# 128 bytes ahead of three phases' buffers, three half tiles instead of four, the last turn inside the third, two more edges of order

## The chip, the cores and the metric

The kernel runs on one core of one Trainium2 chip. The metric is the device time of one execution in microseconds, the median over several runs. A core has a matrix engine (TensorE; PE in the profile, with its weight loads as PEld), a vector engine (VectorE, DVE), a scalar engine (ScalarE, ACT), GpSimd (POOL), and a sync engine (SP), which here issues all loads and stores. Each engine works through a queue of its own in a fixed order, and semaphores hold the queues together.

## The reference

A trunk of two layers for 512 tokens of 1024 channels, all in float32. Layer 0 mixes tokens with a Mamba-2 state space mixer, layer 1 with HGRN2. Behind either mixer stand a layer norm, a squared-ReLU MLP of 4096 hidden channels, another layer norm and a gated input of per-layer embeddings:

```python
for i in range(DEPTH):
    mix = ssd_mixer(x, ...) if i % 2 == 0 else hgrn2_mixer(x, ...)
    h = layer_norm(DEEPNORM_ALPHA * x + mix, ln_g[i, 0], ln_b[i, 0])
    h = layer_norm(DEEPNORM_ALPHA * h + sq_relu_mlp(h, mlp_w1[i], mlp_w2[i]), ln_g[i, 1], ln_b[i, 1])
    x = h + jax.nn.sigmoid(h @ ple_w_gate[i]) * (p[i] @ ple_w_proj[i])

def sq_relu_mlp(h, w1, w2):
    a = jax.nn.relu(h @ w1)
    return (a * a) @ w2
```

In the mixer of layer 0, `u @ w_in` gives the columns x (16 tiles of 128 channels), z (16 tiles), B, C and dt; x, B and C pass a causal convolution of width 4 and a silu before the chunked state computation.

## The kernel before

**Products in three passes.** A float32 product is made of three matmuls in a faster float32 mode. Both factors are split into a high part, rounded by ScalarE (`nc.scalar.copy`), and a low part, the rest, taken by VectorE (`tensor_sub`). `mm3` (lines 117 to 120) issues high by high, high by low and low by high. A weight tile of 128x1024 is loaded by SP into one of three `raw` buffers and split into one of six `whi` and one of six `wlo` buffers; `unit` (line 101) does the load and `split` (108) the rest. The trace names the operand that moves through the array first and the one that is held in it second: `pj<-b,whi` moves an activation past held weights (`project`, line 135), `pj<-whi,b` moves weights past a held activation, 128 tokens of it at a time (`out_part`, `product`, the gate). `pj`, `py`, `pt` and `pm` are the banks of PSUM.

**Buffers.** The pools lie in SBUF in the order in which they are opened: constants, `raws`, `whip`, `wlop`, `b8`, `accp`, `w4`, `sm`, and behind them the pool of the phase (`begin`, line 74), whose buffers are replaced at each of the four phases ssd, mlp0, hgrn and mlp1. The buffers of `raws`, `whip`, `wlop` and `w4` hold 4096 bytes in each partition, those of `b8` 8192, `acc` 16384, so all of these start at the same remainder of 4096. The small tiles of `sm` take 640 bytes (one name of 2x64 and eight of 2x32), and the phase's first buffer begins right behind them. In the two MLP phases it is `blk`, two buffers of 8192 bytes that hold the activation blocks `s3` and `s4`; the other five blocks (`a11`, `a12`, `a22`, `s1`, `s2`) lie in `b8`.

**MLP.** `mlp_and_gate` works on the hidden channels in four groups `g`. `hidden(g)` makes 16 tiles of them in two rounds `p` and lays the squared activations down in seven blocks for a product by Strassen's scheme; `block_product` (337) multiplies these with sums of the second weight matrix (`weight_sums`, 313, buffers `r`). Seven products of 24 matmuls belong to a group; two of the seven (`p7` and `p3`) hold `s3` and `s4`.

**From mixer to MLP in layer 0.** `out_project` with `spread` interleaves the last projection of the mixer with the layer norm of the four chunks of 128 tokens (`layer_norm`, 197, ending with line 213 on VectorE) and with the turn of each chunk (`transpose_split`, 215): eight transposes on TensorE (222), two casts on ScalarE (227), two subtractions on VectorE (228). Chunks 0 and 1 are turned inside `out_project`. Chunks 2 and 3 are handed on as `turns`: the first four tiles of the MLP (`g == p == 0`) are projected for tokens 0 to 255 alone, the turn of chunk 2 follows behind the second of these halves and that of chunk 3 behind the fourth, and then the four second halves follow for tokens 256 to 511.

**What sets the order.** A list scheduler orders each engine's queue when the program is built, by the order of the program text, by priorities (`tc.high_priority`) and by its own estimate of times. TensorE's order in the mixers is written out by hand (`manual_schedule`). `behind(ins)` (97) adds an edge of order: what the block issues on the engine of `ins` comes behind `ins` in that engine's queue. No semaphore belongs to it, and instructions of the block on other engines are free. `marks["pe"]` is the last matmul that was issued, `marks["norm", 0]` the last VectorE instruction of the latest chunk's layer norm.

**The start of layer 0.** `x_part(j)` (625) projects column tile j of x, passes it through `conv_silu` (577: ScalarE's line 580, three additions on VectorE in line 583, a silu on ScalarE in line 586) and keeps the last addition in `conv[j][0]`. Behind tiles x0, z0, x1 and z1, `turn_pair(0)` (646, transposes in line 652) needs the silu of tiles 0 and 1. Then `x_part(2)` follows on TensorE.

Of the kernel before, what the change touches and what calls it, by code (L numbers as in the profile page):

```python
# [15 lines left out]
P = 128  # L16
T = 512
# [24 lines left out]
def trunk(ctx: ExitStack, tc, a):  # L42
    nc = tc.nc
# [14 lines left out]
    uid, marks = [0], {}  # L58
# [16 lines left out]
    def begin(name):  # L75

        if phase:
            phase[1].__exit__(None, None, None)
            phase.clear()
        phase.append(tc.tile_pool(name=name, bufs=1, reuse_waits="tile"))  # L80
        phase.append(phase[0].__enter__())
        phase.reverse()
        phase.append(bufs[name])

    def tmp(tag, shape, dt=F32):
        return mk(phase[0], shape, tag, dt, bufs=phase[2].get(tag, 1))
# [11 lines left out]
    def behind(ins):  # L98
        return nullcontext() if ins is None else tc.issue_after(ins.ins)
# [17 lines left out]
    def mm3(out, sh, sl, mh, ml, start, stop, **kw):  # L117
        nc.tensor.matmul(out, sh, mh, start=start, stop=False, **kw)  # L118
        nc.tensor.matmul(out, sh, ml, start=False, stop=False, **kw)  # L119
        marks["pe"] = nc.tensor.matmul(out, sl, mh, start=False, stop=stop, **kw)  # L120
# [11 lines left out]
        def l(self, k, sl=slice(0, T)):  # L132
            return self.lo[k // 4][:, k % 4, sl]

    def project(src, xs, ps, m=P, tok=slice(0, T)):

        hi, lo = src
        for k in range(8):
            c = slice(k * m, (k + 1) * m)
            mm3(ps[:m, tok], hi[:, c], lo[:, c], xs.h(k, tok), xs.l(k, tok), k == 0, k == 7)  # L140


    begin("ssd")
# [243 lines left out]
    def mlp_and_gate(layer, h_s, last, turns=()):  # L387

        w1, w2 = a[f"w1_{layer}"], a[f"w2_{layer}"]
        blocks = {}  # L390

        def hidden(g):
            names = ("a11", "a12", "a22", "s1", "s2", "s3", "s4")
            blocks[g] = {
                n: tmp("blk", [P, 2, 4, 256], F32R) if n in ("s3", "s4") else mk(b8, [P, 2, 4, 256], "b8", F32R)
                for n in names
            }
            for p in range(2):
                tiles = [4 * (2 * g + r) + 2 * p + i for r in range(2) for i in range(2)]
                us = []  # L400
                if g == p == 0:
                    for i, m in enumerate(tiles):
                        us.append((unit(w1[m]), bank(psj, "pj")))
                        project(us[-1][0], h_s, us[-1][1], tok=slice(0, 256))
                        if turns and i % 2:
                            with behind(marks["pe"]):
                                turns[i // 2]()
                zs = []
                for r in range(2):
                    z = mk(w4, [P, 2, T], "ab"[r])  # L410
                    for i in range(2):
                        if us:
                            u, ps = us[2 * r + i]
                            project(u, h_s, ps, tok=slice(256, 512))
                        else:
                            ps = bank(psj, "pj")
                            with behind(marks["norm", 0] if (layer, g, p, r, i) == (0, 0, 1, 0, 0) else None):
                                u = unit(w1[tiles[2 * r + i]])
                            project(u, h_s, ps)
                        nc.scalar.activation(z[:, i], ps, AF.Relu)  # L420
                        if i == 1:
                            nc.scalar.activation(z, z, AF.Square)
                            zs.append(z)
                            if r == 1:
                                half_blocks(blocks[g], *zs, p)
                        yield

        for g, period in enumerate(PERIODS):
            if g < 4:
                tiles = hidden(g)  # L430
            if g > 0:
                if g == 4:
                    h_s, after, turned, sums = norm(2 * layer + 1)
                    p_s = (mk(w4, [P, 2, T], "a", F32R), mk(w4, [P, 2, T], "b", F32R))
                    praw = mk(raws, [P, 1024], "raw")
                    nc.sync.dma_start(praw, a[f"pT_{layer}"].rearrange("p k t -> p (k t)"))
                    praw = praw.rearrange("p (k t) -> p k t", k=2)
                    nc.scalar.copy(p_s[0], praw)
                    nc.vector.tensor_sub(p_s[1], praw, f32(p_s[0]))
                w = [[[w2[8 * g - 8 + 4 * i + 2 * j + u] for u in range(2)] for j in range(2)] for i in range(2)]  # L440
                products = block_product(w, blocks.pop(g - 1), SUMS[g - 1], g == 1, *((after, lambda: turned(0), sums) if g == 4 else ()))
            for op in period:
                next(tiles if op == "T" else products)

        x_n = None if last else Split(8)
        late = []

        def turn(h, c):

            sl = slice(c * P, (c + 1) * P)  # L450
            pt = bank(psm, "pm") if c % 2 else bank(pst, "pt")
            for j in range(4):
                nc.tensor.transpose(pt[:, j * P : (j + 1) * P], acc[:, c, h * 512 + j * P : h * 512 + (j + 1) * P], ident)
            v = pt.rearrange("p (j t) -> p j t", j=4)
            hh = x_n.hi[h][:, :, sl]
            nc.scalar.copy(hh, v)
            nc.vector.tensor_sub(x_n.lo[h][:, :, sl], v, f32(hh))

        pps = {}

        def proj(c, pu):

            pp = pps[c] = bank(*((psj, "pj") if c > 1 and pps else (psy, "py%d" % (c % 2))))
            for k in range(2):
                ks = slice(k * 512, (k + 1) * 512)
                mm3(pp, p_s[0][:, k, c * P : (c + 1) * P], p_s[1][:, k, c * P : (c + 1) * P], pu[0][:, ks], pu[1][:, ks], k == 0, k == 1)

        for h in range(2):
            pu = unit(a[f"wp_{layer}"][h])
            gu = [unit(a[f"wg_{layer}"][4 * h + j]) for j in range(4)]  # L470
            for c in range(NCH):
                sl = slice(c * P, (c + 1) * P)
                if h == c == 0:
                    for i in range(NCH):
                        proj(i, pu)
                        if i == 1:
                            turned(1)
                if h == 1:
                    proj(c, pu)
                pp = pps.pop(c)  # L480
                pg = bank(psj, "pj")
                sg = tmp("sg", [P, T])
                parts = 2 if last and h == 1 and c == NCH - 1 else 1
                for i in range(parts):
                    n = 512 // parts
                    if i:
                        pg = bank(psj, "pj")
                    cs = slice(i * n, (i + 1) * n)
                    for k in range(8):
                        ks = slice((k % 2) * 512 + i * n, (k % 2) * 512 + (i + 1) * n)  # L490
                        mh, ml = gu[k // 2][0][:, ks], gu[k // 2][1][:, ks]
                        mm3(pg[:, cs], h_s.h(k, sl), h_s.l(k, sl), mh, ml, k == 0, k == 7)
                        if h == 0 and c < 2 and k == 2:
                            turned(c + 2)
                    nc.scalar.activation(sg[:, cs], pg[:, cs], AF.Sigmoid)
                    nc.vector.tensor_mul(sg[:, cs], pp[:, cs], sg[:, cs])
                    fs = slice(h * 512 + i * n, h * 512 + (i + 1) * n)
                    d = acc[:, c, fs]
                    nc.vector.tensor_add(d, sg[:, cs], d)
                    if last:  # L500
                        nc.sync.dma_start(a["out"][c * P : (c + 1) * P, fs], d)
                while late:
                    late.pop(0)()
                if not last:
                    late.append(lambda h=h, c=c: turn(h, c))
        return x_n, late
# [3 lines left out]
    ps = bank(psj, "pj")  # L510
# [79 lines left out]
    def projected(i):  # L590

        if i < 2:
            return first[i]
        ps = bank(psj, "pj")
        project(unit(wssd[i - 2]), x_s, ps)
        return ps
# [26 lines left out]
    prep, live, decay, pair, conv = {}, {}, {}, {}, {}  # L623

    def x_part(j):
        ps = projected(10 * (j // 4) + 2 + 2 * (j % 4))
        xs = tmp("xs", [P, T])
        conv[j] = conv_silu(ps, j, xs)
        live[j] = [xs]
# [135 lines left out]
    with tc.manual_schedule(engines={mybir.EngineType.PE}):  # L765
# [8 lines left out]
        for k in range(1, 9):  # L774
            i, j = 2 * k, 2 * k + 1
# [540 lines left out]
```

## Time and profile before

| | us |
|---|---|
| median of 3 runs | 1421.09 (1419.85 to 1421.74) |
| the profiled execution | 1420.3 |
| its span, first to last instruction | 1418.4 |
| TensorE busy | 1412.2 |
| VectorE busy | 1019.1 |
| ScalarE busy | 741.7 |

A group's row in the profile gives line, engine, operation, tiles and shape, the count, the busy time in us and the mean record of one instruction in ns. Records of matmuls overlap their successors, since the array is pipelined: what one matmul costs is the distance from its start to the next one's start, which is read in the timeline, whose rows begin with a start and a length in us.

### The profile page before, as it was taken

To read this page: it belongs to the slowest core of one execution; us is meant where nothing else is said; L and a number is where in the kernel's file an instruction comes from. 1 tells how busy PE (TensorE), PEld (TensorE's weight loads), DVE (VectorE), ACT (ScalarE), POOL (GpSimd) and SP (SyncE) were. 2 spreads that over 40 slices of the span, in tenths; PEclk is the share of its full clock that TensorE was granted. 3 is DMA by queue.
4 is the path that set the end of the run, shared out by engine and by line. 5 is a ranking of instruction groups with operands and counts; after the bars stand their busy time and mean duration, and the time that the engine had idled before them with its cause. 6 is when DMAs were issued, how large, how long until landed. Compare 5 with 4: busy or idle time off the path is not lost.

```text
span 1418.4 us, 20300 instructions
## 1 busy us (share of the span) xinstructions
PE 1412.2 (100%) x8063; PEld 1181.4 (83%) x8063; DVE 1019.1 (72%) x1677; ACT 741.7 (52%) x1099; POOL 1.5 (0%) x8
## 2 busy tenths in 40 slices
PE   9999999999999999999999999999999999999998
PEld 7888888888988888888888888888898888888887
DVE  7997777695877667687854775676785857666873
ACT  7786566473464444545533446465554454544551
POOL 0000000000000000000000000000000000000000
PEclk9999999999999999999999999999999999999999
DMA  8524333322444444442422322221263444444231
GB/s 296 167 84 134 108 101 119 105 93 102 169 131 146 142 141 141 141 140 98 156 83 92 105 90 74 85 96 63 74 223 111 150 140 142 141 138 160 89 119 45
DMA packets 48958, 174.81 MB, mean 123 GB/s; under 512 B 5728, under 2 KB 6368, under 8 KB 48736
## 3 DMA queue, kind: packets, MB, share of 16 engines
q1 hardware_dynamic: 48864, 173.52, 36.7%
q8 instruction: 63, 1.03, 0.3%
q14 instruction: 31, 0.25, 0.1%
HBM read 171.34 MB, written 2.16 MB: 122 GB/s over the span
## 4 chain that ended last, share of the span: by engine, by line
PE 97%; DVE 1%; DMA 1%; ACT 1%; issue 0%; SPq 0%; ACTq 0%
PE pj L118 25%; PE pj L119 25%; PE pj L120 25%; PE py L118 5%; PE py L119 5%; PE py L120 5%; PE py L709 1%; PE py L975 1%; PE py L711 1%; PE pt L222 1%; PE pt L692 0%; PE pm L222 0%; DVE cv L583 0%; DMA raw<-in_wssd 0%; DMA acc<-in_xw 0%
## 5 line engine op out<-in xcount | busy, mean ns | idle before, releaser
L112 ACT CAST whi<-raw 128x1024 fp32r<-128x1024 f32 x226 | 236.9, 1050 | 386.0 <-PE pj L119 270.3
L114 DVE TENSOR_TENSOR wlo<-raw,whi 128x1024 fp32r<-128x1024 f32 x226 | 274.1, 1220 | 194.5 <-ACT whi L112 191.8
L118 PE MATMUL pj<-b,whi 128*128 128x512 f32 (+1 forms) x1008 | 381.1, 379 | 0.2 <-ACT b L227 0.2
L119 PE MATMUL pj<-b,whi 128*128 128x512 f32 (+1 forms) x1008 | 378.9, 376 | 0.0
L120 PE MATMUL pj<-b,wlo 128*128 128x512 f32 (+1 forms) x1008 | 378.8, 376 | 0.0
L120 PE MATMUL pj<-whi,b 128*128 128x512 f32 (+1 forms) x592 | 229.1, 387 | 0.0
L118 PE MATMUL pj<-whi,b 128*128 128x512 f32 (+1 forms) x584 | 228.8, 392 | 0.0
L119 PE MATMUL pj<-wlo,b 128*128 128x512 f32 (+1 forms) x584 | 226.0, 387 | 0.0
L120 PEld LDWEIGHTS pj<-b,wlo 128*128 128x128 f32 x1008 | 189.7, 188 | 34.4
L118 PEld LDWEIGHTS pj<-b,whi 128*128 128x128 f32 x1008 | 189.5, 188 | 34.6 <-ACT b L227 0.5
L119 PEld LDWEIGHTS pj<-b,whi 128*128 128x128 f32 x1008 | 189.8, 188 | 34.2 <-DVE b L228 0.2
L120 PEld LDWEIGHTS pj<-whi,b 128*128 128x128 f32 x592 | 111.2, 188 | 22.8 <-DVE b L1170 0.2
L118 PEld LDWEIGHTS pj<-whi,b 128*128 128x128 f32 x584 | 109.7, 188 | 23.1 <-ACT k L904 0.4
L119 PEld LDWEIGHTS pj<-wlo,b 128*128 128x128 f32 x584 | 109.8, 188 | 21.3
L112 ACT CAST whi<-r 128x1024 fp32r<-128x1024 f32 x64 | 67.2, 1050 | 64.9 <-PE pj L120 36.8
L114 DVE TENSOR_TENSOR wlo<-r,whi 128x1024 fp32r<-128x1024 f32 x64 | 78.0, 1219 | 22.2 <-ACT whi L112 22.2
L120 PE MATMUL py<-whi,b 128*128 128x512 f32 x216 | 84.1, 389 | 0.0
L119 PE MATMUL py<-wlo,b 128*128 128x512 f32 x192 | 74.7, 389 | 0.0
L118 PE MATMUL py<-whi,b 128*128 128x512 f32 x192 | 74.4, 389 | 0.0
L583 DVE SCALAR_TENSOR_TENSOR cv<-pj,cst,cv 128x509 f32<-128x509 f32 (+2 forms) x66 | 48.8, 741 | 0.4
L120 PEld LDWEIGHTS py<-whi,b 128*128 128x128 f32 x216 | 40.5, 188 | 8.5
L119 PEld LDWEIGHTS py<-wlo,b 128*128 128x128 f32 x192 | 36.0, 188 | 7.5
(338 smaller groups left out, 1805.3 us busy)
## 6 DMA issues: line engine op xcount, KB each, us to landing
raw<-in_w SPq DMA_DIRECT2D x112, 512.0 KB, 3.3
r<-in_w SPq DMA_DIRECT2D x64, 512.0 KB, 3.6
raw<-in_wssd SPq DMA_DIRECT2D x38, 512.0 KB, 4.2
a<-csd SPq DMA_DIRECT2D x16, 512.0 KB, 3.7
raw<-in_wso SPq DMA_DIRECT2D x16, 512.0 KB, 4.3
raw<-in_wg SPq DMA_DIRECT2D x16, 512.0 KB, 3.4
raw<-in_whvg SPq DMA_DIRECT2D x16, 512.0 KB, 3.4
raw<-in_whq SPq DMA_DIRECT2D x16, 512.0 KB, 3.3
```

Source lines behind the costliest of these rows:

```text
L112: nc.scalar.copy(hi[:, :n], f)
L114: nc.vector.tensor_sub(lo[:, :n], f, f32(hi[:, :n]))
L118: nc.tensor.matmul(out, sh, mh, start=start, stop=False, **kw)
L119: nc.tensor.matmul(out, sh, ml, start=False, stop=False, **kw)
L120: marks["pe"] = nc.tensor.matmul(out, sl, mh, start=False, stop=stop, **kw)
L222: nc.tensor.transpose(pt[:, j * P : (j + 1) * P], src[:, k * P : (k + 1) * P], ident)
L583: got = nc.vector.scalar_tensor_tensor(cv[:, d:], ps[:, : T - d], convw[:, i, k : k + 1], cv[:, d:], ALU.mult, ALU.add)
L709: nc.tensor.matmul(yd[64 * r : 64 * r + 64, sl], xdt[:, c, r, :], m[:, r, sl], start=True, stop=c == 0)
L711: nc.tensor.matmul(yd[64 * r : 64 * r + 64, sl], pv[:, c - 1, r, :], ecs[:, r, (c - 1) * P : c * P], start=False, stop=True,)
L975: nc.tensor.matmul(ps[r][32 * b : 32 * b + 32, base + n * c : base + n * c + n], kk[r][:, ts], moving(r, 4 * c + b), start=True, stop=True,)
```

## The change

```diff
@@ begin
         phase.append(bufs[name])
+        if name != "ssd":
+            nc.gpsimd.memset(tmp("pad", [P, 32]), 0.0)
@@ project
-    def project(src, xs, ps, m=P, tok=slice(0, T)):
+    def project(src, xs, ps, m=P, tok=slice(0, T), hook=None, turn=None):
...
             mm3(ps[:m, tok], hi[:, c], lo[:, c], xs.h(k, tok), xs.l(k, tok), k == 0, k == 7)
+            if k == hook:
+                turn()
@@ hidden
-                    for i, m in enumerate(tiles):
+                    for i, m in enumerate(tiles[: 3 if turns else 4]):
                         us.append((unit(w1[m]), bank(psj, "pj")))
-                        project(us[-1][0], h_s, us[-1][1], tok=slice(0, 256))
-                        if turns and i % 2:
-                            with behind(marks["pe"]):
-                                turns[i // 2]()
+                        hook = lambda: None
+                        if turns and i != 1:
+
+                            def hook():
+                                with behind(marks["pe"]):
+                                    turns[i // 2]()
+
+                        project(us[-1][0], h_s, us[-1][1], tok=slice(0, 256), hook=(7, 0, 2, 0)[i], turn=hook)
...
-                        if us:
+                        if len(us) > 2 * r + i:
                             u, ps = us[2 * r + i]
                             project(u, h_s, ps, tok=slice(256, 512))
                         else:
                             ps = bank(psj, "pj")
-                            with behind(marks["norm", 0] if (layer, g, p, r, i) == (0, 0, 1, 0, 0) else None):
+                            with behind(marks["norm", 0] if (layer, g) == (0, 0) and not (p and r) else None):
                                 u = unit(w1[tiles[2 * r + i]])
                             project(u, h_s, ps)
@@ x_part
-        ps = projected(10 * (j // 4) + 2 + 2 * (j % 4))
+        with behind(conv[1][0] if j == 2 else None):
+            ps = projected(10 * (j // 4) + 2 + 2 * (j % 4))
```

- **Pad.** In mlp0, hgrn and mlp1 a tile of 128 bytes in each partition is the first of the phase's pool, so all of the phase's buffers start 128 bytes later. GpSimd fills it with zeros.
- **Halves.** In layer 0 three first tiles, not four, are made in halves; the fourth is made in one pass over all 512 tokens behind them. Layer 1, which hands on no `turns`, keeps four.
- **Turns.** The turn of chunk 2 follows behind the first half tile; that of chunk 3 is asked for inside the third, behind the matmuls of its third k.
- **Edges.** The low part of the weights of x tile 2 comes behind the last convolution addition of x tile 1 on VectorE; `project` of that tile is inside the block too, but no other instruction of it runs on VectorE. In the first group of layer 0, the low parts of the fourth tile of round 0 and of the second tile of round 1 come behind the last norm, as that of the first tile of round 1 did.

## The prediction

> **What bounds the kernel.** First the profile's page, its head and its chain of waits.
>
> ```profile
> span 1418.4 us, 20300 instructions
> PE 1412.2 (100%) x8063; PEld 1181.4 (83%) x8063; DVE 1019.1 (72%) x1677; ACT 741.7 (52%) x1099; POOL 1.5 (0%) x8
> PE 97%; DVE 1%; DMA 1%; ACT 1%; issue 0%; SPq 0%; ACTq 0%
> ```
>
> TensorE is never at rest for long and its own queue is 97% of the chain. So nothing that VectorE, ScalarE or the loads save counts by itself. There are two ways to gain: fewer or shorter matmul slots, or the few places where TensorE waits. I therefore read the groups of instructions by line next, shapes kept apart, and then the timeline of the stages that the change touches.
>
> ```profile
> L118 PE MATMUL pj<-b,whi 128*128 128x512 f32 x880 | 345.2, 392 | 0.0
> L119 PE MATMUL pj<-wlo,b 128*128 128x512 f32 x568 | 221.4, 390 | 0.0
> L119 PE MATMUL py<-wlo,b 128*128 128x512 f32 x192 | 74.7, 389 | 0.0
> L119 PE MATMUL py<-wlo,a 128*128 128x512 f32 x24 | 9.4, 390 | 0.0
> L118 PE MATMUL py<-whi,blk 128*128 128x512 f32 x64 | 25.3, 396 | 0.0
> ...
> L120 PE MATMUL pj<-whi,blk 128*128 128x512 f32 x64 | 25.2, 395 | 0.0
> ```
>
> A matmul that moves 512 columns is on record for 389 to 390 ns, whether the held operand lies in `b8` or in `w4` (named a), and whether the result goes to `pj` or `py`. (392 in the first row has interruptions in it.) Where the held operand lies in `blk`, it is 395 to 396: the two rows are the first and the last of six of 64 each, 384 matmuls in all. Records overlap; the slots are in the timeline of PE:
>
> ```profile
> 368.47 0.28 PE L118 MATMUL pj<-b,whi 128*128 128x256 f32 x1
> ...
> 371.35 0.28 PE L118 MATMUL pj<-b,whi 128*128 128x256 f32 x1
> ...
> 395.37 0.39 PE L118 MATMUL pj<-b,whi 128*128 128x512 f32 x1
> ...
> 400.81 0.39 PE L118 MATMUL pj<-b,whi 128*128 128x512 f32 x1
> ...
> 459.30 0.40 PE L118 MATMUL pj<-whi,blk 128*128 128x512 f32 x1
> 459.54 0.40 PE L119 MATMUL pj<-wlo,blk 128*128 128x512 f32 x1
> ...
> 464.89 0.39 PE L118 MATMUL pj<-b,whi 128*128 128x512 f32 x1
> ```
>
> The first and second row, the third and fourth, and the fifth and last each enclose 24 slots. The plain slot is (400.81 - 395.37) / 24 = 0.2267 us. With `blk` it is (464.89 - 459.30) / 24 = 0.2329, with the longest single slot at 0.24. A half tile's slot, 256 columns, is 2.88 / 24 = 0.120.
>
> **The halves.** In one tile, 24 pairs of half slots become 24 full slots: 24 x (2 x 0.120 - 0.2267) = 0.32 us less on the path, since these matmuls stand back to back. I take **-0.32**. By the Trainium skill, page "TensorE: Matmul & The Clock Gate", section "Back-to-back issue gap", a slot would be N/2.4 + 2.5 ns, a pair of halves would cost only 2.5 ns more than a full one, and this term would be -0.06; the trace shows 13 ns for the pair, and it decides.
>
> **The last turn.** The rows of PE around the turns of chunks 2 and 3, then those of ACT and DVE that belong to them:
>
> ```profile
> 374.23 0.60 PE L222 MATMUL pt<-cst,acc 128*128 128x128 f32 x4
> ...
> 375.02 0.36 PE L118 MATMUL pj<-b,whi 128*128 128x256 f32 x1
> 375.22 0.29 PE L119 MATMUL pj<-b,whi 128*128 128x256 f32 x1
> ...
> 380.85 0.60 PE L222 MATMUL pt<-cst,acc 128*128 128x128 f32 x4
> 381.28 0.60 PE L222 MATMUL pm<-cst,acc 128*128 128x128 f32 x4
> 382.12 0.74 PE L118 MATMUL pj<-b,whi 128*128 128x256 f32 x4 [0.24 <-ACT b L227]
> 382.85 0.39 PE L119 MATMUL pj<-b,whi 128*128 128x256 f32 x1
> 383.07 0.28 PE L120 MATMUL pj<-b,wlo 128*128 128x256 f32 x1
> ```
>
> ```profile
> 369.81 1.28 DVE L213 SCALAR_TENSOR_TENSOR acc<-acc,lnrs,b 128x1024 f32<-128x1024 f32 x1
> ...
> 372.86 0.16 DVE L208 TENSOR_TENSOR lnmv<-lnsq 128x1 f32<-128x1 f32 x1 [0.52 <-ACT cv L205]
> ...
> 374.33 1.28 DVE L213 SCALAR_TENSOR_TENSOR acc<-acc,lnrs,b 128x1024 f32<-128x1024 f32 x1
> ...
> 382.10 0.69 DVE L228 TENSOR_TENSOR b<-pt,b 128x512 fp32r<-128x512 f32 x1 [3.02 <-ACT b L227]
> 382.71 0.68 DVE L228 TENSOR_TENSOR b<-pm,b 128x512 fp32r<-128x512 f32 x1
> ```
>
> The turn of chunk 2 costs 0.79 us to the next matmul and 0.08 in that matmul's slot (0.20 for 0.12). That of chunk 3 costs 1.27; four slots then take 0.73 in place of 0.48, and the next 0.22 in place of 0.12. The surplus is 0.48 + 0.25 - 0.08 + 0.10 = 0.75 us: the second halves stand right behind this turn and wait for its cast and subtractions, which end at 382.71 + 0.68 = 383.39, that is 2.54 us after the turn began.
>
> After the change half tiles and turns follow so: tile 0 from 368.47 to 371.35; turn 2, 0.87; tile 1, 2.88; nine matmuls of tile 2, 1.08, to 376.18; turn 3; fifteen matmuls of tile 2, 1.80. The second halves start at about 378.9, 2.7 us after turn 3 begins, which covers the 2.54. So the old wait goes. What is late next is the norm. Turn 2 is asked for at 371.35, and chunk 2 is ready at 369.81 + 1.28 = 371.09: it just fits. Turn 3 is asked for at 376.18, 4.67 us earlier than before. Chunk 3 was ready at 374.33 + 1.28 = 375.61, but now the two subtractions of turn 2 (0.69 + 0.68) come in front of it on VectorE, of which the idle 0.52 before line 208 takes a part: 375.61 + 1.37 - 0.52 = 376.46. That is a new wait of 0.3, if the scheduler keeps the place; if it sees the wait, it lays matmuls of tile 2 ahead, for which there is room. Bounds: -0.75 (no new wait) and +1.4 (1.37 in full on VectorE, as much again for turn 2's casts in front of chunk 3's squares on ScalarE, and nothing laid ahead: 375.61 + 2.74 = 378.35, a wait of 2.17). I take **-0.45**. The low part of the fourth tile, which the edge puts behind the norm, is read only after three second halves, 8.6 us later, and costs nothing; its cover would have to shrink by that much. That of round 1 is read later still. Both hold their `raw` buffer until then, so the loads behind them wait; before, two low parts stood behind the norm already.
>
> **The edge at the start.** The timeline of PE, DVE and ACT, and a row of SP's waits (between 20 and 45 us):
>
> ```profile
> 41.83 0.60 PE L652 MATMUL py<-cst,xs 128*128 128x128 f32 x4
> 42.85 0.66 PE L652 MATMUL pj<-cst,xs 128*128 128x128 f32 x4 [0.43 <-ACT xs L586]
> ```
>
> ```profile
> 32.90 1.21 DVE L114 TENSOR_TENSOR wlo<-raw,whi 128x1024 fp32r<-128x1024 f32 x1
> ...
> 35.27 1.23 DVE L114 TENSOR_TENSOR wlo<-raw,whi 128x1024 fp32r<-128x1024 f32 x1 [1.15 <-ACT whi L112]
> ...
> 38.20 0.74 DVE L583 SCALAR_TENSOR_TENSOR cv<-pj,cst,cv 128x510 f32<-128x510 f32 x1
> 40.19 1.23 DVE L114 TENSOR_TENSOR wlo<-raw,whi 128x1024 fp32r<-128x1024 f32 x1 [1.25 <-ACT whi L112]
> 41.34 0.74 DVE L583 SCALAR_TENSOR_TENSOR cv<-pj,cst,cv 128x511 f32<-128x511 f32 x1
> ```
>
> ```profile
> 42.17 0.63 ACT L586 ACTIVATE xs<-cv 128x512 f32<-128x512 f32 x1 [0.25 <-DVE cv L583]
> SPq L105 <- DVE wlo L114: 13.5, 7, 4.7
> ```
>
> The transposes of `turn_pair(0)` start at 41.83 and 42.85; four take 0.43 (380.85 to 381.28 holds four of the same kind), so TensorE lost 1.02 - 0.43 = 0.59 us waiting for the silu of x tile 1. That came late because its third addition, ready at 38.94, stood until 41.34 behind a low part whose weights had not landed. In VectorE's queue the low parts follow in the order of the text: at 32.90 stands that of x tile 2, at 35.27 that of x tile 3, and the blocking one is that of the next group's C. With the edge, the one at 32.90 goes behind the third addition. Its `raw` buffer is free later, so the load that waited for it (SP's row: loads wait for low parts) starts later, and the low part that blocked the addition has less reason to stand ahead of it. If it drops behind, the additions end at 38.94 + 0.74 = 39.7, the silu 0.63 later at 40.3, before the transposes at 41.83; the low part of tile 2 then ends at about 40.9, and TensorE wants it at 42.7. The edge adds no semaphore, so nothing behind it in the queue waits longer than for the work in front. Bounds: -0.59, and +2.4, worked out below. I take **-0.59**.
>
> **The pad.** The buffers of `whi`, `wlo`, `b8` and `w4` start at one remainder of 4096. `blk` starts 640 bytes behind it, 2.5 x 256; with the pad 768, 3 x 256. Held slices are 512 bytes, so those of `b8` and `w4` lie 0 (of 512) from the moving operand's start and cost 0.2267; those of `blk` lie 128 and cost 0.2329; after, 256. No row shows 256. If only being whole multiples of 256 apart matters, 384 x 6 ns = 2.3 us go. If the distance has to be a multiple of 512, nothing is gained, or something lost: with each slot as long as the longest single one, 384 x (0.240 - 0.2329) = +2.7. The near row is the plain one, since `a`, which lies just under the phase's buffers, is plain as well: that speaks for the distance and against the place in memory. I take **-2.3**, without certainty. The three memsets run on GpSimd, busy 1.5 us in all, with no reader; behind them in its queue stand only the memsets of hgrn's score buffers, used long after. All three later phases move together, so which buffer follows which old one changes only between ssd and mlp0, under this stage's row, where TensorE rests nowhere:
>
> ```profile
> 400.00:695.00 295.00, 295.00 (x1298) 243.40 (x1297) 210.79 (x254) 146.91 (x186) 0.53 (x1) 1.00 0.41 133
> ```
>
> **Sum.** -0.32 - 0.45 - 0.59 - 2.3 = -3.66. On the profiled execution, 1420.3, this gives 1416.6; that one lies 0.8 under the median 1421.09, from which it gives **1417.4**.
>
> **The rivals.**
>
> *The pad does nothing*: the slot of `blk` comes from its place, not its distance. Then -1.36 remains: 1419.7. For it speaks that the trace has only two distances; against it the row of `a`. Chance 0.22. The Trainium skill, page "SBUF — State Buffer", section "Who interferes with whom", gives TensorE two independent read ports and says "PE and ACT never wait on anyone"; by that rule no address could matter and this rival would hold, while the rows of 395 and 389 ns differ for one shape, which the rule leaves unexplained.
>
> *The pad makes it worse*, the slower end: half a period away is the worst place, and all 384 slots in p7 and p3 of both layers grow. At 0.240 the sum is -1.36 + 2.7: 1422.4. It decides against the change from 1.36 / 384 = 3.5 ns above 0.2329 on, 0.2364. For: 128 is worse than 0, and the trend may go on. Chance 0.09.
>
> *The edge pins the low part behind a late addition*: the load of the blocking tile started when the low part of x tile 2 had freed its buffer, at 32.90 + 1.21 = 34.11. Now it waits for that of x tile 3, 35.27 + 1.23 = 36.50, and is 2.39 late; if the scheduler still puts its low part ahead of the third addition, the wait grows by 2.39 in place of falling by 0.59: 1417.4 + 2.98 = 1420.4. Against: the scheduler then sees a later load and has an idle VectorE in front of it. Chance 0.12.
>
> *The last turn stays where it was*, because the scheduler finds chunk 3 not ready: only the halves' gain and what the shorter queue brings; 1417.9, within the forecast's own range, which holds 0.57.
>
> **How the numbers follow.** About 0.2%, 2.8 us, is what a measurement of this kernel can tell from no change. Faster by more means below 1418.3: nearly all of the forecast case (0.55 of its 0.57). Same holds the idle pad, the pinned edge and a weaker forecast. Slower needs above 1423.9: the worse pad with slots over 0.244, or two mishaps. So 0.55, 0.39 and 0.06. The range, 1416.0 to 1420.8, holds forecast, idle pad and pinned edge and leaves out the worse pad and the tails; the forecast's own range is 1416.4 to 1418.3.
>
> **What would show it.** In the groups by line, the rows of `blk` at 389 to 390 (forecast), 395 (idle pad) or above 400 (worse). In the timeline, 112 half slots of each line in place of 128, no gap of TensorE behind the turn of chunk 3, and at 42 us eight transposes 0.11 apart. The forecast is wrong if the row of `blk` stays, or if a new gap stands before line 222 or line 652.

## The result and the profile after

| | before | after |
|---|---|---|
| median | 1420.77 us (9 runs, 1419.53 to 1422.37) | 1416.96 us (9 runs, 1415.87 to 1417.73) |
| the profiled execution | 1420.3 | 1416.96 |
| its span | 1418.4 | 1415.2 |

The ratio is 0.9973, with a 95% interval of 0.9963 to 0.9983: 3.8 us faster, with an interval of 2.4 to 5.3. The head of the page of the kernel after, and its chain of waits:

```profile
span 1415.2 us, 20254 instructions
...
PE 1409.0 (100%) x8039; PEld 1179.7 (83%) x8039; DVE 1018.4 (72%) x1677; ACT 744.7 (53%) x1101; POOL 1.9 (0%) x11
...
PE 98%; ACT 1%; DMA 0%; DVE 0%; issue 0%; SPq 0%
```

TensorE still sets the time; its busy time fell by 3.2 us, as the span did. VectorE's busy time is the same within 0.1%, and the memsets are what GpSimd gained. The groups by line of the kernel after, shapes kept apart (line 118 of before is 120 now):

```profile
L121 PE MATMUL pj<-b,whi 128*128 128x256 f32 x112 | 31.8, 284 | 0.0
...
L122 PE MATMUL pj<-whi,blk 128*128 128x512 f32 x64 | 25.1, 392 | 0.0
L121 PE MATMUL pj<-wlo,blk 128*128 128x512 f32 x64 | 24.9, 389 | 0.0
...
L121 PE MATMUL py<-wlo,blk 128*128 128x512 f32 x64 | 24.9, 389 | 0.0
```

The half slots are 112 to a line, not 128. The rows of `blk` have fallen from 395 or 396 to 389 (the first row has an interruption in it). Then the timeline of TensorE of the kernel after, at the places that the prediction named:

```profile
42.31 0.60 PE L661 MATMUL py<-cst,xs 128*128 128x128 f32 x4
42.75 0.60 PE L661 MATMUL pj<-cst,xs 128*128 128x128 f32 x4
...
356.60 0.66 PE L226 MATMUL pt<-cst,acc 128*128 128x128 f32 x4 [0.23 <-DVE acc L217]
...
376.60 0.28 PE L122 MATMUL pj<-b,wlo 128*128 128x256 f32 x1
376.92 0.63 PE L226 MATMUL pt<-cst,acc 128*128 128x128 f32 x4
...
377.74 0.37 PE L120 MATMUL pj<-b,whi 128*128 128x256 f32 x1
...
379.25 0.76 PE L120 MATMUL pj<-b,whi 128*128 128x256 f32 x4
379.84 0.28 PE L121 MATMUL pj<-b,whi 128*128 128x256 f32 x1
...
458.64 0.39 PE L120 MATMUL pj<-whi,blk 128*128 128x512 f32 x1
...
464.08 0.39 PE L120 MATMUL pj<-b,whi 128*128 128x512 f32 x1
```

- At 42 us eight transposes follow each other without a gap: the wait of 0.59 is gone.
- At 356 us there is a wait that the kernel before did not have, for the norm of chunk 0.
- The slot at 376.60 is 376.92 - 376.60 = 0.32 long instead of 0.12: a new wait of 0.20 ahead of the last turn, now inside the third tile. Twelve matmuls of that tile stand ahead of it, not the nine behind which it is asked for: the scheduler laid three more there.
- Four half slots from 379.25 on take 0.59 in place of 0.48: a wait of 0.11 is left where the second halves start. The matmul at 379.84 is the first of them that reads a low part.
- With `blk`, 24 slots take 464.08 - 458.64 = 5.44 us, 0.2267 each, where before they took 5.59.

The same places on VectorE in the kernel after, and then its ScalarE at the start of layer 0:

```profile
39.40 2.31 DVE L591 SCALAR_TENSOR_TENSOR cv<-pj,cst,cv 128x509 f32<-128x509 f32 x3 [5.30 <-ACT cv L588]
41.63 3.49 DVE L116 TENSOR_TENSOR wlo<-raw,whi 128x1024 fp32r<-128x1024 f32 x3
...
353.34 1.28 DVE L216 SCALAR_TENSOR_TENSOR acc<-acc,lnmv,a 128x1024 f32<-128x1024 f32 x1 [0.29 <-DVE lnmv L212]
...
375.49 1.29 DVE L217 SCALAR_TENSOR_TENSOR acc<-acc,lnrs,b 128x1024 f32<-128x1024 f32 x1
376.69 2.35 DVE L116 TENSOR_TENSOR wlo<-raw,whi 128x1024 fp32r<-128x1024 f32 x2
378.96 0.68 DVE L232 TENSOR_TENSOR b<-pt,b 128x512 fp32r<-128x512 f32 x1
```

```profile
37.64 1.05 ACT L114 CAST whi<-raw 128x1024 fp32r<-128x1024 f32 x1 [2.82 <-DMA raw<-in_wssd]
38.59 0.77 ACT L588 ACTIVATE cv<-pj,cst 128x512 f32<-128x512 f32 x1
...
41.81 0.63 ACT L594 ACTIVATE xs<-cv 128x512 f32<-128x512 f32 x1 [1.51 <-DVE cv L591]
```

At the start the three additions of x tile 1 now stand together, and all three low parts behind them. At 353.34 VectorE pauses for 0.29 us ahead of the first line of the norm, behind an instruction of its own that was done; in the kernel before this row (line 212) has no pause, and the transposes of chunk 0 no wait:

```profile
353.14 1.28 DVE L212 SCALAR_TENSOR_TENSOR acc<-acc,lnmv,a 128x1024 f32<-128x1024 f32 x1
```

```profile
356.41 0.66 PE L222 MATMUL pt<-cst,acc 128*128 128x128 f32 x4
```

Laid side by side, start by start, the matmuls of the profiled execution after stand so against those of before (a difference of two starts each, minus is earlier):

| stage | at its end | change |
|---|---|---|
| the first 20 us | +0.49 | +0.49 |
| the start of layer 0, to 43 us | -0.16 | -0.65 |
| the mixer of layer 0, to 356 us | -0.16 | 0 |
| the turn of chunk 0 | +0.19 | +0.35 |
| halves and last two turns, to 395 us | -0.65 | -0.84 |
| from there to the end | -3.22 | -2.57 |

The first row is no work of the change: up to 20 us every engine does the same work in the same order in the two kernels, and in the other profiled executions below the same difference lies between -0.35 and +0.90.

### The profile page after: what moved, and what is told of

The parts are those of the page before. It is cut to its first block, busy times and chain, and to the rows that moved or that the text cites. A ratio compares the mean times of both kernels' runs of the same rounds, so it can differ in the third digit from the quotient of the medians.

```text
span 1415.2 us, 20254 instructions
## 1 busy us (share of the span) xinstructions
PE 1409.0 (100%) x8039; PEld 1179.7 (83%) x8039; DVE 1018.4 (72%) x1677; ACT 744.7 (53%) x1101; POOL 1.9 (0%) x11
## 4 chain that ended last, share of the span: by engine, by line
PE 98%; ACT 1%; DMA 0%; DVE 0%; issue 0%; SPq 0%
PE pj L120 26%; PE pj L122 25%; PE pj L121 25%; PE py L120 5%; PE py L121 5%; PE py L122 5%; PE py L718 1%; PE py L984 1%; PE py L720 1%; PE pt L226 1%; PE pm L226 0%; PE pt L701 0%; DMA acc<-in_xw 0%; PE pt L661 0%; PE pt L1153 0%; PE pm L1153 0%
## 5 line engine op out<-in xcount | busy, mean ns | idle before, releaser
L122 PE MATMUL pj<-whi,b 128*128 128x512 f32 (+1 forms) x592 | 229.1, 387 | 0.0
L122 PEld LDWEIGHTS py<-whi,b 128*128 128x128 f32 x216 | 40.5, 188 | 8.5
L120 PEld LDWEIGHTS py<-whi,b 128*128 128x128 f32 x192 | 36.0, 188 | 7.6
```

## The experiments

**One part at a time.** The theory is that of the prediction: four gains in four places that add, -2.3 of them from the distance of `blk`. The rivals were that the pad does nothing, and that the rest is lost in new waits. The four kernels ran together, with 33 runs of the kernel before (1420.76).

*The pad alone* (against the kernel before):

```diff
         phase.append(bufs[name])
+        if name != "ssd":
+            nc.gpsimd.memset(tmp("pad", [P, 32]), 0.0)
```

> The kernel before with the pad alone. Theory (distance): a held slice that lies 128 (of 256) bytes from the moving operand's start costs 6 ns a slot, one that lies a multiple of 256 away nothing, so the six rows of blk fall from 395-396 to 389-390 ns and the time by 2.3 us, to about 1418.5; the waits at 42 us (0.59) and behind the turn of chunk 3 (0.75) stay. Rival (order): the gain came from the reshuffled queues, and the pad by itself changes neither the rows of blk nor the time: 1420.8.

Measured: 1418.29 (11 runs), ratio 0.9983 (0.9975 to 0.9992), that is -2.47 us. Its groups by line, and its PE timeline at 42 us:

```profile
L120 PE MATMUL pj<-whi,blk 128*128 128x512 f32 x64 | 24.9, 389 | 0.0
...
L121 PE MATMUL py<-wlo,blk 128*128 128x512 f32 x64 | 24.9, 389 | 0.0
```

```profile
41.47 0.60 PE L654 MATMUL py<-cst,xs 128*128 128x128 f32 x4
42.77 0.66 PE L654 MATMUL pj<-cst,xs 128*128 128x128 f32 x4 [0.70 <-ACT xs L588]
```

The slots are short and the old wait stands. The pad is the larger part of the gain and needs none of the other edits.

*The change without the pad*:

```diff
-        if name != "ssd":
-            nc.gpsimd.memset(tmp("pad", [P, 32]), 0.0)
```

> The changed kernel without the pad. Distance: the rows of blk are back at 395-396, and 1.5 us of the 3.8 remain: about 1419.3. Order: the rows stay as in the changed kernel, and so does the time, 1417.

Measured: 1419.57 (11 runs), ratio 0.9992 (0.9983 to 1.0001), -1.19 us, which the interval does not quite tell from nothing. The rows of `blk` are back at 395 and 396:

```profile
L118 PE MATMUL pj<-whi,blk 128*128 128x512 f32 x64 | 25.3, 396 | 0.0
...
L120 PE MATMUL pj<-whi,blk 128*128 128x512 f32 x64 | 25.3, 395 | 0.0
```

*The edge on x tile 2 alone* (against the kernel before):

```diff
-        ps = projected(10 * (j // 4) + 2 + 2 * (j % 4))
+        with behind(conv[1][0] if j == 2 else None):
+            ps = projected(10 * (j // 4) + 2 + 2 * (j % 4))
```

> The kernel before with the edge on x tile 2 alone. Theory: the wait ahead of the second four transposes of turn_pair(0) at 42 us goes (0.59 to 0), the rest stays, 1420.2. Rival (pinned): the blocking low part still stands ahead of the third addition, and the wait grows to about 3 us: 1423.

Measured: 1420.49 (11 runs), ratio 0.9996 (0.9987 to 1.0004), -0.27 us, not to be told from nothing. Its VectorE and its PE around the turn of chunk 0:

```profile
353.13 1.28 DVE L212 SCALAR_TENSOR_TENSOR acc<-acc,lnmv,a 128x1024 f32<-128x1024 f32 x1 [0.29 <-DVE lnmv L208]
```

```profile
356.40 0.66 PE L222 MATMUL pt<-cst,acc 128*128 128x128 f32 x4 [0.23 <-DVE acc L213]
```

The wait at 42 us is gone in this kernel (-0.64 us between 41 and 43.5 us, start by start), and 0.37 us of it is given back at 356 us. So the new wait at the turn of chunk 0 comes with this edge, 310 us behind the place where it works, and not with the turns.

*Halves, turns and the edges in the MLP alone*, that is the change without the pad and without the edge on x tile 2 (the two diffs above taken back):

> The kernel before with the three half tiles, the earlier turns and the edges behind the norm, without pad and without the edge on x tile 2. Theory: 0.32 from the halves and 0.45 from the last turn, so about 0.8 less, 1420.0, with the wait at 42 us in place and a wait of about 0.3 ahead of the turn of chunk 3. Rival: the wait only moved from behind that turn to ahead of it, so that no more than the 0.32 is left, 1420.5.

Measured: 1419.97 (11 runs), ratio 0.9995 (0.9986 to 1.0004), -0.79 us, by time alone not to be told from nothing either; start by start the stage from 365 to 395 us is 0.84 shorter, as in the whole change, and nothing else moves. The old wait at 42 us stands. The parts by their medians, -2.47 - 0.27 - 0.79 = -3.53, add up to the -3.81 of the whole within what the intervals leave open.

**Why the pad works: distance or place.** Four kernels with 20 runs of the kernel before (1421.22). In the first three only the size of the pad is another:

```diff
-            nc.gpsimd.memset(tmp("pad", [P, 32]), 0.0)
+            nc.gpsimd.memset(tmp("pad", [P, 64]), 0.0)
```

> The changed kernel with 256 bytes of pad in place of 128: blk then starts 896 bytes behind the remainder of whi, 3.5 x 256, so a held slice lies 128 (of 256) from the moving operand's start, as without a pad, while the place in memory has moved on. Theory (distance of 256): the rows of blk are back at 395-396 ns and the time rises by 2.3 us, to about 1419.3. Rival (place): any move away from the old start helps, the rows stay at 389 and the time at 1417.

```diff
-            nc.gpsimd.memset(tmp("pad", [P, 32]), 0.0)
+            nc.gpsimd.memset(tmp("pad", [P, 96]), 0.0)
```

> The changed kernel with 384 bytes of pad: blk starts 1024 bytes behind the remainder of whi, 4 x 256. Theory (distance of 256): as with 128 bytes, rows at 389-390 and 1417. Place would say the same; a theory by which only the old distance of 640 was bad as well. It tells the theories apart only together with the 256 and the 64 bytes.

```diff
-            nc.gpsimd.memset(tmp("pad", [P, 32]), 0.0)
+            nc.gpsimd.memset(tmp("pad", [P, 16]), 0.0)
```

> The changed kernel with 64 bytes of pad: 704 bytes behind the remainder of whi, 2.75 x 256, so 192 (of 256) from the moving operand's start. Distance theory in its strict form (only multiples of 256 are plain): rows of blk above 390, anywhere up to 396 and time between 1417 and 1419.5. In a form where only the opposite half (128 of 256) is bad: rows at 389, 1417.

| pad | `blk` behind the old remainder | from a whole 256 | mean slot of `blk` | time | ratio |
|---|---|---|---|---|---|
| 0 (before) | 640 | 128 | 232.9 ns | 1421.22 | |
| 64 | 704 | 64 | 229.0 | 1417.37 (9 runs) | 0.9975 (0.9966 to 0.9985) |
| 128 (after) | 768 | 0 | 226.8 | 1416.96 | 0.9973 (0.9963 to 0.9983) |
| 256 | 896 | 128 | 232.9 | 1419.52 (10 runs) | 0.9989 (0.9979 to 0.9998) |
| 384 | 1024 | 0 | 226.8 | 1416.92 (6 runs) | 0.9969 (0.9958 to 0.9981) |

The row of 128 bytes is that of the section on the result, where the kernel before stood at 1420.77. The mean slot is that of the 382 to 384 matmuls with `blk`, from start to next start. The groups by line with 256, with 384 and with 64 bytes:

```profile
L120 PE MATMUL pj<-whi,blk 128*128 128x512 f32 x64 | 25.3, 396 | 0.0
...
L121 PE MATMUL py<-wlo,blk 128*128 128x512 f32 x64 | 25.3, 395 | 0.0
```

```profile
L121 PE MATMUL py<-wlo,blk 128*128 128x512 f32 x64 | 24.9, 389 | 0.0
```

```profile
L121 PE MATMUL py<-wlo,blk 128*128 128x512 f32 x64 | 25.2, 394 | 0.0
...
L122 PE MATMUL py<-whi,blk 128*128 128x512 f32 x64 | 24.8, 388 | 0.0
```

A buffer pushed further along is slow again, and further still fast again: it is where the buffer starts modulo 256 bytes, not how far along it lies, and 512 need not be met (128 bytes of pad leave 768, 384 leave 1024, and both are fast). A quarter of the period costs about a third of what half of it costs, 2.2 of 6.1 ns; this is a mean of rows that differ, 231.6 where `wlo` is moved, and 229.1 and 226.3 in the two lines that move `whi`.

*The same distance for everything*: 128 bytes between the weights' buffers and all that follows, so that `b8`, `w4` and the phase's buffers all lie 128 from `whi` and `wlo`:

```diff
     wlop = pool("wlop", 6)
+    gap = pool("gap", 1)
     b8 = pool("b8", 9)
...
+    nc.gpsimd.memset(mk(gap, [P, 32], "gap"), 0.0)
     begin("ssd")
```

> The changed kernel with 128 bytes between the pools of wlo and b8, so that b8, w4 and the phase's buffers all lie 128 (of 256) bytes off the split weights. Theory (distance): now nearly all of the big matmuls are off, and their rows go from 389-390 to 395-396; 888 x 3 moving b8, 568 x 3 and 200 x 3 holding b8 and 64 x 6 holding blk are about 5350 slots, and at 6 ns this is 32 us more: about 1449. Rival (place): the rows stay and the time stays at 1417.

Measured: 1446.7 (4 runs), ratio 1.018 (1.0165 to 1.0195), some 30 us above the whole change. Its groups by line:

```profile
L121 PE MATMUL pj<-b,whi 128*128 128x512 f32 x888 | 352.9, 397 | 0.0
L122 PE MATMUL pj<-b,whi 128*128 128x512 f32 x888 | 350.5, 395 | 0.0
...
L122 PE MATMUL pj<-b,whi 128*128 128x256 f32 x112 | 31.6, 283 | 0.0
```

Every row of 512 columns is now at 395 or above, whether the moving operand lies in `b8` or in the weights (mean slots 232.7 both); some 5,400 slots by 5.7 ns (the difference of their means) are 31 us, where 32 had been expected. The rows of 256 columns stayed at 283, and their slots at 119, in the median, against 120. So neither `blk` nor the MLP is special: `b8` and the weights pay the same, at 512 columns.

In all these kernels `whi` and `wlo` stay in place, so a buffer's distance from them and its own remainder of 256 change together, and the rows above do not tell these two apart. A shorter row does. Seven times in the mixer of layer 1 a matmul of 128 columns (`pt<-a,sc`, `pt<-a,btok`, `pt<-b,btok`), with one operand in `w4` or `b8` and the other in the phase's pool, follows one of 512 columns. Its slot is 113 or 114 ns in the kernel before and with 256 bytes of pad, and 108 or 109 with 64, 128 and 384. In the kernel with the gap both its operands lie 128 bytes further along than in the whole change, at the same distance from each other: six of the seven are at 108 or 109, one at 114. So for these the distance counts, and not the remainder of a buffer by itself.

Nor is it only the distance of a matmul's own two operands. The 16 matmuls that stand just ahead of a product with `blk` have both operands in plain places, and they took 232.5 ns in the kernel before and 226.5 in the whole change. What their slot shares with the slow ones is that the next matmul holds `blk`. How the reading of two operands comes to cost this time, no run shows.

**The places where the change left something.** Four kernels, with 19 runs of the kernel before (1420.89).

*Four places down VectorE's queue.* In every kernel so far with the edge on x tile 2 the row with the pause stands at place 575 of VectorE's queue, counted from 0 and with its semaphore instructions; in the kernels without the edge the same instruction stands at 579 and has no pause. The edge takes four semaphore instructions out of the queue ahead of it.

```diff
+    for _ in range(4):
+        nc.vector.memset(lbr, 0.0)
     nc.vector.reciprocal(lbr, lb0)
```

> The whole change, and four tiny memsets of a 128x8 tile on VectorE near the start of the kernel, so that everything behind them in VectorE's queue stands four places later; no other engine's queue changes. Theory (the 0.27 to 0.29 us that VectorE pauses ahead of chunk 0's norm belong to a place in its queue, the 575th instruction, where the norm's first line stands in every kernel with the edge on x tile 2 and in none without it): the norm's line now stands at 579, its pause is gone (under 0.05), the transposes of chunk 0 at about 356 us wait under 0.05 for it instead of 0.23, the pause shows at another, earlier instruction, and the time is 0.2 to 0.3 us under that of the whole change, 1416.7. Rival (the pause belongs to the work around it, as the edge has ordered it): pause and wait stay at 0.29 and 0.23, and the time stays at 1416.9 or 0.1 above it for the memsets.

Measured: 1416.84 (7 runs), ratio 0.9972 (0.9961 to 0.9983). VectorE and PE at the turn of chunk 0:

```profile
353.11 0.16 DVE L212 TENSOR_TENSOR lnmv<-lnsq 128x1 f32<-128x1 f32 x1 [1.59 <-ACT cv L209]
353.19 1.28 DVE L216 SCALAR_TENSOR_TENSOR acc<-acc,lnmv,a 128x1024 f32<-128x1024 f32 x1
```

```profile
356.46 0.66 PE L226 MATMUL pt<-cst,acc 128*128 128x128 f32 x4
```

The pause and TensorE's wait are gone, and start by start the turn of chunk 0 costs nothing against the kernel before (+0.05 ahead of it and +0.05 behind), where the whole change loses 0.35 there. So the work by itself does not make the pause: it comes with the place of this work in the queue. That it would show at another instruction instead was wrong, for the rows around place 575 have no pause now. A pause there could be hidden, though. In the whole change 0.42 us pass from the end of the semaphore instruction ahead of the norm's line to that line, here 0.04; and at place 575 there now stands the read of an accumulator, 0.68 us behind the start of the instruction of 0.75 us that it reads from, long enough to cover it. No run shows whether it does. The gain is there in the trace; the time, 0.12 under the whole change's, cannot show it, since the first 20 us alone differ by more.

*The last turn asked for two k later*. In TensorE's queue it comes one k later, three matmuls, since the scheduler had laid it behind the fourth k in the whole change:

```diff
-                        project(us[-1][0], h_s, us[-1][1], tok=slice(0, 256), hook=(7, 0, 2, 0)[i], turn=hook)
+                        project(us[-1][0], h_s, us[-1][1], tok=slice(0, 256), hook=(7, 0, 4, 0)[i], turn=hook)
```

> The whole change with the turn of chunk 3 asked for behind the fifth k of the third tile in place of the third k. In TensorE's queue the transposes come three matmuls (0.36 us) later, and nothing else changes. Theory (TensorE waits 0.20 us ahead of this turn for VectorE's norm of chunk 3, which ends at about 376.8): the long slot of 0.32 ahead of the turn is gone (0.12), the second halves still find their cast and subtractions done, and everything behind is 0.2 us earlier: 1416.7. Rival (the second halves then wait for the turn's subtractions, as they did before the change, since only three fewer half slots stand in between): a wait on ACT or VectorE appears at the first matmul of the second halves, 0.2 to 0.4, and the time stays at 1416.9 to 1417.1.

Measured: 1417.07 (7 runs), ratio 0.9972 (0.9962 to 0.9983). Its PE, and its VectorE:

```profile
376.52 0.28 PE L122 MATMUL pj<-b,wlo 128*128 128x256 f32 x1
376.64 0.60 PE L226 MATMUL pt<-cst,acc 128*128 128x128 f32 x4
...
378.58 0.75 PE L120 MATMUL pj<-b,whi 128*128 128x256 f32 x4
379.25 0.39 PE L121 MATMUL pj<-b,whi 128*128 128x256 f32 x1
379.48 0.28 PE L122 MATMUL pj<-b,wlo 128*128 128x256 f32 x1
```

```profile
375.04 1.28 DVE L217 SCALAR_TENSOR_TENSOR acc<-acc,lnrs,b 128x1024 f32<-128x1024 f32 x1
376.25 2.35 DVE L116 TENSOR_TENSOR wlo<-raw,whi 128x1024 fp32r<-128x1024 f32 x2
378.51 0.68 DVE L232 TENSOR_TENSOR b<-pt,b 128x512 fp32r<-128x512 f32 x1
```

The slot ahead of the turn is 0.12, as expected, but where the second halves start the slots are longer by (379.25 - 378.58 - 0.48) + (0.23 - 0.12) = 0.30, where the whole change had 0.11. The rival was right: the wait moved. What stays is VectorE's stretch from the end of the norm to the first low part that TensorE reads: 379.84 - (375.49 + 1.29) = 3.06 us in the whole change and 379.25 - (375.04 + 1.28) = 2.93 here, with another 0.11 of wait behind it. In it stand the two low parts of weights, 2.35 us, ahead of the turn's subtraction: the two that the new edges put behind the norm.

*Both together*:

> The whole change with both edits: the four memsets on VectorE and the turn of chunk 3 behind the fifth k. If both theories hold the two gains of 0.2 to 0.3 and 0.2 add: 1416.5. If only one holds, 1416.7; if neither, 1416.9 to 1417.1. In the timeline of TensorE no wait over 0.05 is left at 356 us and none at 376 us in the first case.

Measured: 1416.77 (7 runs), ratio 0.9971 (0.996 to 0.9982). Its PE at the last turn:

```profile
376.35 0.60 PE L226 MATMUL pt<-cst,acc 128*128 128x128 f32 x4
...
378.30 0.75 PE L120 MATMUL pj<-b,whi 128*128 128x256 f32 x4
378.97 0.38 PE L121 MATMUL pj<-b,whi 128*128 128x256 f32 x1
```

The wait at 356 us is gone as with the memsets alone, the one at 376 us has moved to the second halves as with the later turn alone (0.67 for four slots in place of 0.48). So one of the two theories holds. This kernel has the lowest median of all, and neither it nor any other can be told from the whole change by time.

*The pad in the first phase too*:

```diff
-        if name != "ssd":
+        if True:
```

> The whole change with the pad of 128 bytes also ahead of the buffers of the first phase (ssd); GpSimd gains one memset and no other queue changes. In this phase the buffers behind the pad lie at 256 of 512 from the whi, wlo and b8 buffers in place of 128. Theory (a matmul's slot depends on the distance of its two operands only where it moves 512 columns): the mixer of layer 0 has few such matmuls with an operand in the phase's pool, so the time stays within 0.5 of 1416.9 and the mixer's rows of 128 columns keep their means. Rival (shorter matmuls pay for the distance too): the mixer's rows with one operand in the phase's pool get shorter, by up to 6 ns each, and the end comes up to 2 us earlier.

Measured: 1417.28 (9 runs), ratio 0.9974 (0.9964 to 0.9984): nothing gained. The 256 matmuls of line 718, 128 columns with the held operand in the phase's pool, have the same mean record as in the whole change (276 ns) and the same mean slot (56.2). (So has line 720, but both its operands lie in the phase's pool, so their distance did not change.) These did not pay for the distance, while the seven in the mixer of layer 1 above did. Nor did the mixer's matmuls of 512 columns all keep their slots: twelve of them stand ahead of a matmul that holds `btok` or `ss` of the phase's pool, and took 233 or 234 ns in the whole change and 228 or 229 here. These 0.06 us do not show at the end: start by start the mixer of layer 0 took 0.2 us longer than in the whole change.

## Why the prediction was right, point by point

The forecast was -3.66 us and the measured change is -3.81; its own case came true, and none of the rivals did. But one of its own signs of being wrong came too, a new gap before line 222 (226 after the change), and twice: 0.20 at 376 us, which it had put at 0.3, and 0.23 at 356 us, which it had put at nothing. The single terms are nearer in some places than in others.

**The pad: -2.3 forecast.** Alone it gave -2.47 by the medians, and -2.55 in the trace from 395 us to the end. The mechanism (whole multiples of 256 apart) was one of several that the rows of before allowed: the pad itself told it from multiples of 512, the pads of 256 and 384 bytes from the place. It is not the whole of it, since the operand that the next matmul holds counts as well. 384 slots by 232.9 - 226.8 = 6.1 ns are 2.34; another 0.20 came between 705 and 1060 us, in the mixer of layer 1, where no `blk` is in use and which was not costed. It goes with the same distance: 0.20 to 0.24 in the traces of all kernels with 128 or 384 bytes (the gap kernel left out), none, within 0.03, with 256 or without a pad. No matmul of 512 columns there has an operand of its own in the phase's pool, but eight stand ahead of one that holds `btok` or `sc`, 233 to 235 ns before and 226 to 229 after, and the seven short ones behind gained 5 each. This is 0.08; the rest lies in slots near these whose operands are all in plain places, and is not traced further.

**The pad as nothing, and the pad as a loss.** Both rivals fell. The row of `a`, on which the forecast leaned, was a good witness: a plain slot in a buffer just below the slow one. The Trainium skill, page "SBUF — State Buffer", section "Who interferes with whom", calls TensorE's two read ports independent and says that "PE and ACT never wait on anyone"; read as the prediction reads it, no address could matter. The kernel with the gap of 128 bytes has 395 ns and more in every row of 512 columns where the whole change has 389, and pays 30 us for it. The measurement decides: whatever holds between engines, TensorE loses time by how its own operands lie to each other.

**Halves and last turn: -0.32 and -0.45 forecast, -0.77 together.** Measured -0.84 in the stage and -0.79 by the medians of the run without pad and edge. The new wait ahead of turn 3 was put at 0.3 and is 0.20, in part by luck: the norm ended at 375.49 + 1.29 = 376.78, the transposes began at 376.92, and without the three matmuls that the scheduler laid ahead (0.36), which the prediction allowed for but did not count, the wait would have been 0.56. The step that failed is a small one: "The low part of the fourth tile, which the edge puts behind the norm, is read only after three second halves, 8.6 us later, and costs nothing". Its reader does wait for nothing, but in VectorE's queue it stands, with that of round 1, ahead of the turn's subtractions, and 0.11 of the old wait is left. The prediction named the queue's order for turn 2's subtractions and not here. The turn that stays where it was, a rival, did not come: turn 3 stands inside the third tile, behind its fourth k.

**The edge at the start: -0.59 forecast.** The wait went, as forecast, in every kernel with this edge (0.65 start by start in the whole change, 0.64 alone). But the term was mis-sized: the run with the edge alone gave -0.27 by the medians, whose interval holds -0.59 as well as 0, and about 0 in its trace, for two reasons that the runs show. The pause of VectorE at the norm of chunk 0 gives 0.35 to 0.37 back. The step that put it at nothing was "The edge adds no semaphore, so nothing behind it in the queue waits longer than for the work in front": 310 us further on VectorE stood for 0.29 us with its work in front done. And the wait had been covering the first 20 us: in the kernels without the edge the projection behind the transposes starts at one time within 0.09 us, whatever came before (43.27 before; the pad alone, 0.35 earlier at 20 us, only 0.08 earlier here), so 0.59 was the size of the wait in one execution, and 0.87 (42.77 - 41.47 - 0.43) in the run of the pad alone; with the edge, what the first 20 us gain or lose goes through (-0.58 to +0.25 at this place, the kernel with the gap left out; 0.64 or 0.65 less than at 20 us in each).

The working had a second error there that cost nothing: the additions were to end at 39.7 and the silu at 40.3. They ended at 41.7 and 42.4, 0.3 before the second set of transposes. In ScalarE's queue the convolution's first step (38.59) now stands behind a cast that waited 2.82 us for its weights, the same kind of wait as the one that the edge removed from VectorE. The cover was 0.3, not 1.5.

**The edge that pins the low part**, a rival: all three low parts follow the additions, and the wait did not grow.

**Sum.** In the trace of the whole change: -0.65 at the edge, +0.35 at the pause, -0.84 for halves and turns, -2.57 behind, together -3.71, and +0.49 of the first 20 us, which is no work of the change, make the -3.22 between the spans. That the forecast of the whole was within 0.15 is in part luck: the edge gave less than its term, and the pad and the halves more.

## What to carry to other kernels

Where one matrix product stands at two durations in the profile for the same shape, group its rows by operand, that of the next matmul too, and put the addresses beside them: here 128 bytes ahead of a pool were worth 2.5 us, and a wrong distance for all buffers cost 30. A wait that ends with a load may have been covering what came before it, so what is removed is worth less than its length in one trace. An edge that delays an instruction must be costed for all that is queued behind it on that engine, not only for its reader.

## What the runs showed of the hardware

- A matmul that moves 512 columns took a slot of 226.8 ns where its two operands start a whole multiple of 256 bytes apart, 229.0 in the mean with 64 bytes from that, and 232.9 with 128; rows of 256 columns stayed as they were (records of 283 ns) when the distance changed.
- It took 232.5 to 234 ns with its own operands in place where the next matmul held an operand 128 bytes off (16 ahead of `blk`, twelve in the mixer of layer 0), and 226.5 to 229 where the distance of that one was made whole. Of the matmuls of 128 columns those of line 718 stayed at 276 ns, and seven behind a long one in the mixer of layer 1 went from 113 or 114 to 108 or 109.
- VectorE paused for 0.27 to 0.29 us ahead of the instruction at place 575 of its queue, with no semaphore that explains it, in each kernel where the norm's first line stood there, and not when four tiny memsets moved that line to place 579. What the chip does at that place, and whether it is only hidden where another instruction stands there, stays open. So does whether the two low parts, put behind the turn's subtractions, would free the last 0.3 us of waits around turn 3: it was not tried.
